# Two low-rank products of a recurrent layer's preparation parted, z tiles evacuated at an earlier due time, and one set of small transfers moved to another queue

## The chip, the cores and the metric

One core of a Trainium2 chip. The metric is the device time of one execution in microseconds (us), as the median of several runs. Engines are named as the profile names them: PE (TensorE: matmuls and transposes), PEld (its weight loads), DVE (VectorE), ACT (ScalarE), POOL (GpSimd) and SP (SyncE, which here only issues transfers). Each engine works through its own list of instructions in order; transfers can be issued from SP, ACT or POOL.

## The reference

A decoder layer for 1024 tokens of width 2048, in float32. One RMS norm feeds one input projection of 6528 columns. Its columns go to two groups of heads:

```python
h = rms_norm(x, norm_w[l], NORM_EPS)
z = h @ w_in[l]
y_rwkv = rwkv7_mixer(z[..., :RWKV_COLS], ...)   # 16 heads x 64
y_att = swa_sink_mixer(z[..., RWKV_COLS:], ...)  # 16 query heads, 2 key heads, window 128
x = x + concat([y_rwkv, y_att]) @ w_out[l]
```

The first group mixes each column with the token before it and then runs a recurrence per head, of which the parts that matter here are

```python
w = -softplus(-(w0 + tanh(wl) @ w2)) - 0.5
decay = exp(-exp(w))
a = sigmoid(a0 + al @ a2)
kk = k * k_k / norm(k * k_k)          # per head
k = k * (1 + (a - 1) * k_a)
# per token t: sa = state @ (-kk)
# state = state * decay + outer(sa, kk * a) + outer(v, k);  o = state @ r
```

`wl` and `al` have 64 columns each: `tanh(wl) @ w2` and `al @ a2` are the two low-rank products of the change.

## The kernel before

The tokens are worked through in two halves of 512 (`hf`). In each half a stream of z tiles is projected: a z tile is 128 output columns by 512 tokens, made in one of two PSUM banks (tag "z") by 48 matmuls of 128x128 by 512, as three products of high and low parts over 16 pieces of the contraction (L346, L347, L351). Weights come in four pieces per tile on SP (L335), are rounded by ACT to the high part `wh` (L321) and subtracted by POOL to the low part `wl` (L322).

A finished z tile is multiplied in its bank by the row norms (L353, DVE). `shifted` then blends it with the token before: ACT L359, DVE L360, ACT L361 and L362 (`zlast`, the last reader of the bank). Only then is the bank free for the tile after the next.

A unit (`unit`, 8 per half, so 16 in all) has six z tiles, in this order: k, r, v and the gate of two recurrent heads (`zk`, `zr`, `zv`, `zg`), then the queries of two attention heads, then the attention's gate. Beside the stream run generators for each unit:

- `rwkv_prep`: the two low-rank products (L390, L391, two matmuls each; the second operand of each is a low part), their tanh on ACT (L393, L394), the decay's cumulated sum `sig` (POOL L395, DVE scan L399) and its exponentials `Pc` and `Pi` (ACT L401, L405), `kmul` (ACT L397), the norm of kk through `headsum` (ACT L552, POOL L553, two matmuls L555 and L556; DVE L409 and the reciprocal L410), then the scaled operands `Gt` (L421, L422) and `F` (L426, L427). Per set of four chunks of 64 tokens 16 small matmuls follow (L436) into two banks; DVE masks them out of the banks into `Eab`, `BE` and `F` (L439, L440, L442). There are two sets, and both use the tag "m".
- `solve`, inside it: the inverse of each 16x16 triangle on DVE (L463, L464), copied out by ACT (L465), put into DRAM in two transfers (L467) and read back in four as larger blocks `dg` (L469), transposed by DVE (L473), and used in small matmuls from L477 to L512. Both sets of transfers are issued on SP.
- `rwkv_chain` (the recurrence over eight chunks, L578 to L589), `rwkv_post` (norm over each head, transposes L616), and `att` (attention of the unit; its last products are L724 and L726 with DVE L731, its output's transposes L735 with DVE L737). These of one unit run beside the next unit's `rwkv_prep`.

PSUM tag "m" has three banks for all of this. In `rwkv_prep` `pw` and `pa`, the banks of the two low-rank products, are taken together and then `pn` for the norm; `pa` is used on until L422.

What sets the order: `yield t` gives the due time of what follows, in planned us, and `at(t)` sets the same as a priority directly. A planner orders each engine's list at build time by due time among what its own cost model holds to be ready; on the chip the lists are fixed. A z tile is planned at 15.36 us (`TILE`), so a unit at 92.16; counted from its start `t0`, the low-rank products are due at 18.5, the norm sum at 23.2, `Gt` and `F` at 32, the L436 and masks at 57.2 (the second set's L436 and masks at 62.4), and a tile's evacuation at the planned end of the tile: 46.08 for `zv` and 61.44 for `zg`.

At the turn from the first half to the second, `hprep` loads, transposes (L287) and splits the second half of x (L262, L263), and the last unit's `solve` stands there without z tiles of the same half beside it. The x loads (L254) and weight loads (L335) are on SP, as L467 and L469.

Of the kernel before, what the change touches and what calls it, by code (L numbers as in the profile page):

```python
# [13 lines left out]
AF = mybir.ActivationFunctionType  # L14
ALU = mybir.AluOpType
# [49 lines left out]
def layer(tc, x, norm_w, w_in, w_out, mu_rwkv, w0, w2, a0, a2, k_k, k_a, r_k, lnx_w, lnx_b,  # L65
          q_norm_w, k_norm_w, sinks, rel_bias, cst, out, groups=range(NP), do_out=True, dbg=None):
    nc = tc.nc
# [5 lines left out]
    V, A, G, PE = nc.vector, nc.scalar, nc.gpsimd, nc.tensor  # L73

    def sb(shape, tag, bufs=1, dt=F32):
        return pool.tile(list(shape), dt, name=tag, tag=tag, bufs=bufs)

    HR = (slice(0, 64), slice(64, 128))
    NT = dict(t=4, ta=5, zt=5, wr=4, wh=3, wl=3)

    def tmp(tag="t"):
        return sb([P, T], tag, NT.get(tag, 1))

    def ps(tag, shape=(P, 512)):
        return psum.tile(list(shape), F32, name=tag, tag=tag, bufs={"z": 2, "m": 3, "o": 1, "ch": 1}[tag])
# [6 lines left out]
    def at(t):  # L92
        tc.cur_priority = 100000 + int(t * 1000)
# [15 lines left out]
    order, now = itertools.count(), [0.0]  # L109
# [42 lines left out]
    def col(name, i=0):  # L152
        return cols(name, 1, i)
# [14 lines left out]
    dv = {}  # L168
# [51 lines left out]
    dg, mp = sb([P, NC, 32], "dg"), sb([P, NC, 32], "mp")  # L220
    V.memset(dg[:], 0.0)
    xd = dram.tile([2, 2, NC, 32, 32], F32, name="xd", tag="xd")
    x5 = xd[:]
# [101 lines left out]
    def ztile(h, c0, c1=None):  # L325

        hh, hl, R = h
        z = ps("z")

        def load(q):  # L330
            def f(raw):
                r3 = raw.rearrange("p (k c) -> p k c", k=4)
                for i, c in ((slice(0, P), c0),) if c1 is None else ((HR[0], c0), (HR[1], c1)):
                    w = w_in[0, q * 512:(q + 1) * 512, c:c + i.stop - i.start]
                    nc.sync.dma_start(r3[:, :, i], w.rearrange("(k p) c -> p k c", p=P))  # L335
            return f

        t0 = clk[0]
        clk[0] += TILE
        for q in range(4):  # L340
            hi, lo = wpiece(load(q), t0 + q * 12 * MM)
            for k in range(4):
                kk = q * 4 + k
                yield t0 + (q * 12 + 2 * k) * MM
                wh = hi[:, k * P:(k + 1) * P]
                PE.matmul(z[:], lhsT=wh, rhs=hh[kk][:], start=(kk == 0), stop=False)  # L346
                PE.matmul(z[:], lhsT=wh, rhs=hl[kk][:], start=False, stop=False)  # L347
            for k in range(4):
                kk = q * 4 + k
                yield t0 + (q * 12 + 8 + k) * MM  # L350
                PE.matmul(z[:], lhsT=lo[:, k * P:(k + 1) * P], rhs=hh[kk][:], start=False, stop=(kk == KT - 1))  # L351
        yield clk[0]
        V.tensor_tensor(z[:], z[:], R[:], ALU.mult)  # L353
        return z

# [10 lines left out]
    def v3(t, n=T):  # L366
        return t.rearrange("p (c t) -> p c t", c=NC)

    def rwkv_prep(t0, hf, p, S, lor, zk, zr, zv):
# [10 lines left out]
        for i in range(2):  # L380
            hr = HR[1 - i]
# [2 lines left out]

        sq = tmp()
        A.activation(sq[:], zk[:, 0:T], AF.Square, scale=col("kk", p))
        pw, pa = ps("m"), ps("m")
        yield t0 + 18.5
        for i, (b, hr) in enumerate(zip((pw, pa), HR)):
            PE.matmul(b[:], lhsT=wla[:, i, :], rhs=lor[i][:], start=True, stop=False)  # L390
            PE.matmul(b[:], lhsT=whz[:, i, :], rhs=lor[2][:], start=False, stop=True)  # L391
        th = tmp()
        A.activation(th[:], pw[:], AF.Tanh, bias=dv["hw0"][:, p:p + 1], scale=0.5)  # L393
        A.activation(pa[:], pa[:], AF.Tanh, bias=dv["ha0"][:, p:p + 1], scale=0.5)  # L394
        G.tensor_scalar(sig[:, :, 1:65], v3(th[:]), 0.5, 0.5, ALU.mult, ALU.add)  # L395
        kmul = tmp()
        A.activation(kmul[:], pa[:], AF.Identity, bias=dv["cka"][:, p:p + 1], scale=dv["hka"][:, p:p + 1])  # L397
        fl = lambda t: t[:].rearrange("p a b -> p (a b)")
        V.tensor_tensor_scan(fl(sig), fl(rmask), fl(sig), 0.0, ALU.mult, ALU.add)  # L399
        Pc = sb([P, NC, 65], "Pc", 1)  # L400
# [2 lines left out]
        A.copy(pe[:], Pc[:, :, 64])  # L403
        Pi = tmp()
        A.activation(v3(Pi[:]), sig[:, :, 1:65], AF.Exp, scale=C0)  # L405
        pn = ps("m")
        yield from headsum(pn, sq, t0 + 23.2)
        n2 = tmp()
        V.tensor_scalar(n2[:], pn[:], 1e-24, None, ALU.max)  # L409
        V.reciprocal(n2[:], n2[:])  # L410
        V.scalar_tensor_tensor(pa[:], pa[:], 1.0, n2[:], ALU.add, ALU.mult)
        k3, r3 = v3(zk[:, 0:T]), v3(zr[:, 0:T])
        kP = Pi
# [37 lines left out]
        Xs = sb([64, 16, 16], "X")  # L451
# [3 lines left out]
        def solve():  # L455
            G.memset(Xs[:].rearrange("p s t -> p (s t)")[:, 0:256:17], 1.0)
            X = chx[0:64, 256:512].rearrange("p (s t) -> p s t", s=16)
            A.copy(X, Xs[:])  # L458
            for j in range(14, 0, -1):
                n = 15 - j  # L460
                yield t0 + 65 + n * 0.35
                q = sb([64, 64], "pr", 2)[:, 0:j * n].rearrange("p (s t) -> p s t", s=j)
                V.tensor_tensor(q, Xs[:, 0:j, j:j + 1].to_broadcast([64, j, n]), X[:, j:j + 1, j + 1:16].to_broadcast([64, j, n]), ALU.mult)  # L463
                V.tensor_tensor(X[:, 0:j, j + 1:16], X[:, 0:j, j + 1:16], q, ALU.add)  # L464
            A.copy(Xs[:], X)  # L465
            for x, h in halves:
                nc.sync.dma_start(x5.rearrange("i b c s t -> (i b c) s t")[:, h, h], Xs[x])  # L467
            for i, b, r, cb in quads:
                nc.sync.dma_start(dg[r], x5[i, b].rearrange("c s t -> s c t"))  # L469

            yield t0 + 77.5
            dt = sb([P, NC, 32], "k1", 2)
            V.transpose(dt[:], dg[:])  # L473
            pm = ps("m", (P, NC, 64))
            for c in range(NC):
                for i, b, r, cb in quads:
                    PE.matmul(pm[r, c, 0:32], lhsT=Eab[r, c, cb], rhs=dt[r, c, :], start=True, stop=True)  # L477
            V.copy_predicated(mp[:], low_i[:, None, :].to_broadcast([P, NC, 32]), pm[:, :, 0:32])
            yield t0 + 80.5
            for c in range(NC):  # L480
                for i, b, r, cb in quads:
                    PE.matmul(pm[r, c, 32:64], lhsT=dg[r, c, :], rhs=mp[r, c, :], start=True, stop=True)
            for i, b, r, cb in quads:
                A.copy(yt[r, :, r], pm[r, :, 32:64])

            yield t0 + 83
            x22 = sb([P, NC, 32], "k1", 2)
            pz = ps("m", (P, NC, 64))
            for c in range(NC):
                for i in range(2):  # L490
                    r0 = i * 64
                    PE.matmul(pz[r0 + 32:r0 + 64, c, 0:32], lhsT=Eab[r0:r0 + 32, c, 32:64], rhs=yt[r0:r0 + 32, c, r0:r0 + 32], start=True, stop=True)
            z1 = sb([P, NC, 32], "k1", 2)
            for i in range(2):
                r = slice(i * 64 + 32, i * 64 + 64)
                V.transpose(x22[r], yt[r, :, r])
                A.copy(z1[r], pz[r, :, 0:32])
            yield t0 + 85.5
            for c in range(NC):
                for i in range(2):  # L500
                    r = slice(i * 64 + 32, i * 64 + 64)
                    PE.matmul(pz[r, c, 32:64], lhsT=x22[r, c, :], rhs=z1[r, c, :], start=True, stop=True)
            for i in range(2):
                r0 = i * 64
                A.copy(yt[r0 + 32:r0 + 64, :, r0:r0 + 32], pz[r0 + 32:r0 + 64, :, 32:64])

            yield t0 + 88.5
            for c0 in (0, 4):
                cc = slice(c0, c0 + 4)
                b = ps("m", (P, 4, P))  # L510
                for c in range(4):
                    PE.matmul(b[:, c, :], lhsT=yt[:, c0 + c, :], rhs=BE[:, c0 + c, :], start=True, stop=True)  # L512
                for i, hr in enumerate(HR):
                    A.copy(bk[hr, cc, hr], b[hr, :, hr])
                    V.tensor_copy(Erb[hr, cc, HR[1 - i]], b[hr, :, HR[1 - i]])
# [4 lines left out]
        for c0 in (0, 4):  # L520
            b = ps("m", (P, 4, P))
# [27 lines left out]
    def headsum(acc, v, t):  # L549

        hi, lo = sb([P, T], "vh", 1, F32R), sb([P, T], "vl", 1, F32R)
        A.copy(hi[:], v[:])  # L552
        G.tensor_tensor(lo[:], v[:], hi[:].bitcast(F32), ALU.subtract)  # L553
        yield t
        PE.matmul(acc[:], lhsT=bonr[:], rhs=hi[:], start=True, stop=False)  # L555
        PE.matmul(acc[:], lhsT=bonr[:], rhs=lo[:], start=False, stop=True)  # L556
# [66 lines left out]

    def att_kv(hf, h):
        z = yield from ztile(h, RWKV_COLS + 1024)
        kz = tmp("ta")
        A.copy(kz[:], z[:])
# [225 lines left out]
    if dbg is not None:  # L853
        for hf in range(NH):
            for k in list(groups) + [NP + g for g in groups]:
                t = tmp()
# [28 lines left out]
```

## Time and profile before

| | |
|---|---|
| Median of 3 runs | 2073.68 us (2072.9 to 2077.31) |
| The profiled execution | 2074.8 us; span of its instructions 2073.0 us |
| PE busy | 1990.7 us (96%) |
| DVE busy | 1138.2 us (55%) |
| ACT busy | 1042.0 us (50%) |
| POOL busy | 858.0 us (41%) |
| Mean granted clock of PE | 0.989 |

The span runs from the first to the last instruction of the profiled execution. Busy times are sums over the engine's instructions. Matmuls overlap in the array, so a busy PE is not PE at its peak; idle time of PE is real. "a <- b" in a wait means that a stood until b had ended.

### The profile page before, as it was taken

To read this page: it belongs to the slowest core of one execution; us is meant where nothing else is said; L and a number is where in the kernel's file an instruction comes from. 1 tells how busy PE (TensorE), PEld (TensorE's weight loads), DVE (VectorE), ACT (ScalarE), POOL (GpSimd) and SP (SyncE) were. 2 spreads that over 40 slices of the span, in tenths; PEclk is the share of its full clock that TensorE was granted. 3 is DMA by queue.
4 is the path that set the end of the run, shared out by engine and by line. 5 is a ranking of instruction groups with operands and counts; after the bars stand their busy time and mean duration, and the time that the engine had idled before them with its cause. 6 is when DMAs were issued, how large, how long until landed. Compare 5 with 4: busy or idle time off the path is not lost.

```text
span 2073.0 us, 36509 instructions
## 1 busy us (share of the span) xinstructions
PE 1990.7 (96%) x13216; PEld 1632.8 (79%) x13216; DVE 1138.2 (55%) x2680; ACT 1042.0 (50%) x2563; POOL 858.0 (41%) x740
## 2 busy tenths in 40 slices
PE   7999999999999998899999999999999988999999
PEld 5778777787778786777878787877887778988887
DVE  5647575757574756676565665757575772011001
ACT  5445555565555564655645464555556562223221
POOL 4543434434353534144443534344343423444443
PEclk9999999999999999899999999999999999999999
DMA  7332323233332325123232324232323353455443
GB/s 181 88 89 65 93 64 82 76 79 75 81 80 77 87 65 153 42 84 82 78 79 64 96 56 100 62 92 68 81 75 78 75 167 121 152 157 171 134 136 117
DMA packets 412293, 197.02 MB, mean 95 GB/s; under 512 B 216941, under 2 KB 381136, under 8 KB 412112
## 3 DMA queue, kind: packets, MB, share of 16 engines
q1 hardware_dynamic: 371360, 181.90, 32.0%
q10 hardware_dynamic: 40000, 11.67, 2.3%
q0 software_dynamic: 752, 1.11, 0.5%
q8 instruction: 104, 1.70, 0.3%
q14 instruction: 77, 0.63, 0.1%
HBM read 173.51 MB, written 21.10 MB: 94 GB/s over the span
## 4 chain that ended last, share of the span: by engine, by line
PE 38%; DVE 9%; issue 3%; POOL 1%; ACT 1%; DMA 1%; SPq 0%; POOLq 0%; ACTq 0%
PE z L346 6%; PE z L347 6%; PE z L351 6%; PE z L787 2%; PE z L789 2%; PE z L788 2%; PE m L789 2%; PE m L788 2%; PE m L787 2%; POOL wl L322 1%; DVE t L410 1%; PE o L789 1%; PE o L788 1%; PE o L787 1%; PE o L578 1%
## 5 line engine op out<-in xcount | busy, mean ns | idle before, releaser
L322 POOL TENSOR_TENSOR wl<-wr,wh 128x512 fp32r<-128x512 f32 x536 | 707.6, 1324 | 979.9 <-ACT wh L321 510.1
L346 PE MATMUL z<-hh,wh 128*128 128x512 f32 x1632 | 665.1, 408 | 9.7 <-ACT zlast L362 7.6
L347 PE MATMUL z<-hl,wh 128*128 128x512 f32 x1632 | 650.4, 398 | 0.0
L321 ACT CAST wh<-wr 128x512 fp32r<-128x512 f32 x536 | 331.2, 619 | 581.9 <-PE z L347 213.6
L351 PE MATMUL z<-hh,wl 128*128 128x512 f32 x1632 | 477.3, 405 | 0.0
L346 PEld LDWEIGHTS z<-hh,wh 128*128 128x128 f32 x1632 | 308.7, 189 | 81.6 <-ACT zlast L362 13.3
L347 PEld LDWEIGHTS z<-hl,wh 128*128 128x128 f32 x1632 | 308.9, 189 | 59.4 <-DVE hl L263 0.3
L351 PEld LDWEIGHTS z<-hh,wl 128*128 128x128 f32 x1632 | 297.4, 189 | 59.3 <-issue 0.2
L353 DVE TENSOR_TENSOR z<-z,R 128x512 f32<-128x512 f32 x102 | 70.9, 695 | 135.4 <-PE z L351 132.0
L787 PE MATMUL z<-wh,hh 128*128 128x256 f32 (+1 forms) x352 | 113.5, 323 | 11.5 <-ACT hh L259 5.8
L581 ACT ACTIVATE s<-svu,pe 64x64 f32<-64x64 f32 x256 | 88.3, 345 | 49.9 <-DVE svu L589 46.1
L788 PE MATMUL z<-wl,hh 128*128 128x256 f32 (+1 forms) x352 | 112.5, 320 | 0.0
L789 PE MATMUL z<-wh,hl 128*128 128x256 f32 (+1 forms) x352 | 112.5, 320 | 0.0
L578 PEld LDWEIGHTS o<-svu,F 128*128 128x128 f32 x512 | 79.7, 189 | 26.4 <-DVE svu L589 16.5
L589 DVE SCALAR_TENSOR_TENSOR svu<-ch,pe,s 64x64 f32<-64x64 f32 x224 | 63.2, 282 | 65.5 <-PE ch L585 61.7
L463 DVE TENSOR_TENSOR pr<-X,ch 64x14 f32<-64x14 f32 (+6 forms) x224 | 42.3, 189 | 99.8 <-ACT ch L458 92.8
L578 PE MATMUL o<-svu,F 128*128 128x64 f32 x512 | 82.7, 265 | 7.6 <-DVE svu L589 7.1
L787 PEld LDWEIGHTS z<-wh,hh 128*128 128x128 f32 x352 | 68.5, 195 | 16.7 <-ACT hh L259 6.2
L795 DVE TENSOR_TENSOR ta<-z,ta 128x256 f32<-128x256 f32 (+1 forms) x22 | 9.9, 493 | 127.6 <-PE z L789 127.6
L795 DVE TENSOR_TENSOR ta<-m,ta 128x512 f32<-128x512 f32 x9 | 6.1, 689 | 124.8 <-PE m L789 124.8
L788 PEld LDWEIGHTS z<-wl,hh 128*128 128x128 f32 x352 | 68.7, 195 | 4.3
L789 PEld LDWEIGHTS z<-wh,hl 128*128 128x128 f32 x352 | 68.6, 195 | 4.3
(278 smaller groups left out, 3351.6 us busy)
## 6 DMA issues: line engine op xcount, KB each, us to landing
wr<-in_w_in SPq DMA_DIRECT2D x280, 256.0 KB, 2.9
wr<-in_w_in SPq DMA_DIRECT2D x256, 128.0 KB, 2.6
wr<-in_w_out SPq DMA_DIRECT2D x64, 256.0 KB, 2.9
wr<-in_w_out SPq DMA_DIRECT2D x128, 128.0 KB, 2.9
ta<-in_x SPq DMA_DIRECT2D x37, 256.0 KB, 5.4
zt<-yd SPq DMA_DIRECT2D x32, 256.0 KB, 3.7
out<-ta SPq DMA_DIRECT2D x24, 256.0 KB, 4.0
yd<-ta ACTq DMA_DIRECT2D x16, 256.0 KB, 3.0
```

The source lines that it names most:

```text
L321: A.copy(hi[:], raw)
L322: G.tensor_tensor(lo[:], raw, hi[:].bitcast(F32), ALU.subtract)
L346: PE.matmul(z[:], lhsT=wh, rhs=hh[kk][:], start=(kk == 0), stop=False)
L347: PE.matmul(z[:], lhsT=wh, rhs=hl[kk][:], start=False, stop=False)
L351: PE.matmul(z[:], lhsT=lo[:, k * P:(k + 1) * P], rhs=hh[kk][:], start=False, stop=(kk == KT - 1))
L353: V.tensor_tensor(z[:], z[:], R[:], ALU.mult)
L578: PE.matmul(O[:, c, i, :], lhsT=F[c // 4][:, i, c % 4, :], rhs=svu[:, i, c, :], start=c % 4 == 0 and i == 0, stop=False, skip_group_check= ...
L581: A.activation(s0[hr], svu[hr, i, c, :], AF.Copy, scale=pe[hr, c:c + 1])
L589: V.scalar_tensor_tensor(dst, ch[hr, i, :], pe[hr, c:c + 1], s0[hr], ALU.mult, ALU.add)
L787: PE.matmul(o, lhsT=yh[k][:, ts], rhs=wh, start=k == 0 and tt % n == 0, stop=False, skip_group_check=True)
L788: PE.matmul(o, lhsT=yh[k][:, ts], rhs=wl, start=False, stop=False, skip_group_check=True)
L789: PE.matmul(o, lhsT=yl[k][:, ts], rhs=wh, start=False, stop=k == KT - 1 and tt % n == n - 1, skip_group_check=True)
```

## The change

The evacuation of every z tile, and what directly follows it, gets a due time 14 us earlier. In `rwkv_prep` the two low-rank products no longer stand together: the first is due at 17.5, then come the norm sum (due at 21.5) with its reciprocal, the scan and the exponentials, and the second product with its tanh and `kmul` is due at 27; each takes its bank at its own place. The transfers L467 and L469 of the last unit of the first half go through POOL's queue in place of SP's.

```diff
@@ ztile
         yield clk[0]
+        at(now[0] - 14)
         V.tensor_tensor(z[:], z[:], R[:], ALU.mult)
@@ rwkv_prep
-        pw, pa = ps("m"), ps("m")
-        yield t0 + 18.5
-        for i, (b, hr) in enumerate(zip((pw, pa), HR)):
+
+        def lora(i):
+            b = ps("m")
             PE.matmul(b[:], lhsT=wla[:, i, :], rhs=lor[i][:], start=True, stop=False)
             PE.matmul(b[:], lhsT=whz[:, i, :], rhs=lor[2][:], start=False, stop=True)
+            return b
+
+        yield t0 + 17.5
+        pw = lora(0)
         th = tmp()
         A.activation(th[:], pw[:], AF.Tanh, bias=dv["hw0"][:, p:p + 1], scale=0.5)
-        A.activation(pa[:], pa[:], AF.Tanh, bias=dv["ha0"][:, p:p + 1], scale=0.5)
         G.tensor_scalar(sig[:, :, 1:65], v3(th[:]), 0.5, 0.5, ALU.mult, ALU.add)
-        kmul = tmp()
-        A.activation(kmul[:], pa[:], AF.Identity, bias=dv["cka"][:, p:p + 1], scale=dv["hka"][:, p:p + 1])
+        pn = ps("m")
+        yield from headsum(pn, sq, t0 + 21.5)
+        n2 = tmp()
+        V.tensor_scalar(n2[:], pn[:], 1e-24, None, ALU.max)
+        V.reciprocal(n2[:], n2[:])
         fl = lambda t: t[:].rearrange("p a b -> p (a b)")
         V.tensor_tensor_scan(fl(sig), fl(rmask), fl(sig), 0.0, ALU.mult, ALU.add)
...
         A.activation(v3(Pi[:]), sig[:, :, 1:65], AF.Exp, scale=C0)
-        pn = ps("m")
-        yield from headsum(pn, sq, t0 + 23.2)
-        n2 = tmp()
-        V.tensor_scalar(n2[:], pn[:], 1e-24, None, ALU.max)
-        V.reciprocal(n2[:], n2[:])
+        yield t0 + 27
+        pa = lora(1)
+        A.activation(pa[:], pa[:], AF.Tanh, bias=dv["ha0"][:, p:p + 1], scale=0.5)
+        kmul = tmp()
+        A.activation(kmul[:], pa[:], AF.Identity, bias=dv["cka"][:, p:p + 1], scale=dv["hka"][:, p:p + 1])
         V.scalar_tensor_tensor(pa[:], pa[:], 1.0, n2[:], ALU.add, ALU.mult)
@@ solve
+            q = nc.gpsimd if hf == 0 and p == groups[-1] else nc.sync
             for x, h in halves:
-                nc.sync.dma_start(x5.rearrange("i b c s t -> (i b c) s t")[:, h, h], Xs[x])
+                q.dma_start(x5.rearrange("i b c s t -> (i b c) s t")[:, h, h], Xs[x])
             for i, b, r, cb in quads:
-                nc.sync.dma_start(dg[r], x5[i, b].rearrange("c s t -> s c t"))
+                q.dma_start(dg[r], x5[i, b].rearrange("c s t -> s c t"))
```

## Rows read from the trace of the kernel before

**Rows 1.** The page's busy us, share of the span, instructions, by engine

```profile
PE 1990.7 (96%) x13216; PEld 1632.8 (79%) x13216; DVE 1138.2 (55%) x2680; ACT 1042.0 (50%) x2563; POOL 858.0 (41%) x740
```

**Rows 2.** Windows of 20 us: length, busy us (instructions), granted clock, DMA share, GB/s

```profile
820.00:840.00 20.00, 7.26 (x203) 5.48 (x203) 3.16 (x6) 5.32 (x14) 2.49 (x2) 0.64 0.43 109
...
1340.00:1360.00 20.00, 18.61 (x107) 14.58 (x106) 18.91 (x37) 7.50 (x16) 7.49 (x7) 1.00 0.40 99
```

**Rows 3.** Waits of PE, whole span: us in total, times, longest us

```profile
PE m L436 <- DVE F L442: 12.4, 20, 1.9
PE m L477 <- DVE k L473: 10.1, 1, 10.1
...
PE z L346 <- ACT zlast L362: 7.6, 13, 0.8
```

**Rows 4.** Timeline of PE, a unit of the second half: start, us, instruction [idle before]

```profile
1328.20 0.48 PE L390 MATMUL m<-lr,wla 128*128 128x512 f32 x1
...
1329.21 0.33 PE L726 MATMUL m<-vt,ta 128*128 128x64 f32 x2
...
1348.80 1.10 PE L351 MATMUL z<-hh,wl 128*128 128x512 f32 x4
1350.19 0.50 PE L346 MATMUL z<-hh,wh 128*128 128x512 f32 x1 [0.29 <-ACT zlast L362]
...
1353.38 1.13 PE L436 MATMUL m<-F,Gt 64*128 64x128 f32 x14 [0.92 <-DVE F L442]
```

**Rows 5.** Timeline of DVE in the same unit

```profile
1332.71 0.42 DVE L731 TENSOR_TENSOR ta<-m,sm 128x256 f32<-128x256 f32 x1 [0.92 <-PE m L726]
...
1336.72 3.35 DVE L410 RECIPROCAL t<-t 128x512 f32<-128x512 f32 x1
...
1347.36 0.70 DVE L353 TENSOR_TENSOR z<-z,R 128x512 f32<-128x512 f32 x1
...
1350.41 0.41 DVE L439 TENSOR_TENSOR Eab<-m,tri 64x256 f32<-64x256 f32 x1
...
1352.55 0.68 DVE L442 TENSOR_TENSOR F<-m,tri 64x512 f32<-64x512 f32 x1
1353.16 0.68 DVE L353 TENSOR_TENSOR z<-z,R 128x512 f32<-128x512 f32 x1
```

**Rows 6.** Timeline of all engines, the last unit of the first half

```profile
791.05 0.70 DVE L353 TENSOR_TENSOR z<-z,R 128x512 f32<-128x512 f32 x1
...
792.51 0.39 ACT L361 ACTIVATE zv<-zlast,zv,par 128x1 f32<-128x1 f32 x1
...
793.37 0.74 DVE L360 SCALAR_TENSOR_TENSOR zv<-z,par,zv 128x511 f32<-128x511 f32 x1
...
794.41 0.50 PE L346 MATMUL z<-hh,wh 128*128 128x512 f32 x1 [0.82 <-ACT zlast L362]
```

**Rows 7.** Timeline of all engines at the turn

```profile
821.61 0.36 ACT L465 COPY X<-ch 64x256 f32<-64x256 f32 x1
...
821.78 2.49 POOL L322 TENSOR_TENSOR wl<-wr,wh 128x512 fp32r<-128x512 f32 x2 [4.02 <-ACT wh L321]
...
823.53 0.99 SPq L467 DMA_DIRECT2D xd<-X  x2
...
826.85 1.81 SPq L469 DMA_DIRECT2D dg<-xd  x4
831.12 0.45 DVE L473 STREAM_TRANSPOSE k<-dg 128x256 f32<-128x256 f32 x1 [8.80 <-DMA dg<-xd]
```

**Rows 8.** Transfers by issuing queue: count, KB each, median us from issue to landing

```profile
dg<-xd SPq DMA_DIRECT2D x64, 32.0 KB, 2.3
...
bias_d<-Eab POOLq DMA_DIRECT2D x1, 1024.0 KB, 12.6
...
xd<-X SPq DMA_DIRECT2D x32, 32.0 KB, 2.8
...
bia<-in_q_norm_w POOLq DMA_DIRECT2D x2, 0.2 KB, 3.4
```

## The prediction

> **What bounds the kernel now.** I read the page's busy times first, then the windows, then TensorE's waits, and last the instructions of one unit and of the turn between the two token halves. TensorE (PE) is busy 1990.7 of 2073.0 us [rows 1], so only its 82 idle us can be won; the change removes no matmul. In a steady 20 us window inside a unit PE lacks 1.4 us, and DVE is at 18.91 of 20 there; in the window of the turn PE is busy 7.26 us and its granted clock is 0.64 on average, so much of it at the lower of the two levels (1.2 instead of 2.4 GHz) while PE stands idle [rows 2]. The waits say where the rest lies: 12.4 us in 20 waits of the second set of chunk products (L436) for a mask on DVE (L442), 10.1 us in one wait of L477 for a transpose on DVE (L473), and 7.6 us in 13 waits of a new z tile for the evacuation of an old one (L362) [rows 3].
>
> In one unit it looks so. PE ends the gate's z tile (zg) at 1349.90, is held 0.29 us before the next tile because the bank of zv is not empty, goes on, and is held again 0.92 us before the L436 that starts at 1353.38 [rows 4]. The other side is DVE: it stood 0.92 us until 1332.71 for PE (L731), then worked without a gap through the reciprocal (3.35 us), evacuated zv only at 1347.36, though PE had long left that tile, reached the masks at 1350.41 and ended them at 1352.55 + 0.68 = 1353.23 [rows 5]. So the end of the second L442 on DVE sets when PE goes on. A unit of the first half has the same shape with a longer z wait, 0.82 us [rows 6].
>
> **The two low-rank products parted.** Before, four matmuls stand together from 1328.20 to 1329.21, 1.01 us, ahead of the rest of the attention product that DVE's L731 waits for [rows 4, 5]. The second pair leaves that place, so L731 and all DVE work chained behind it can start about 0.5 us earlier. The pair itself costs the same 0.5 us of PE wherever it stands: no gain, no loss in PE work. Its tanh and kmul on ACT come later; they are needed by L411 and L421, which stand behind the reciprocal, and its 3.35 us hide them (the tanh and the affine step are under 1 us each). If that cover were gone, L421 would be about 1 us late and the masks with it. The norm sum and its reciprocal move ahead of the scan in the text; DVE has no gap between them before, so this is an exchange within one full engine and I cost it at nothing; it could give up to the 0.92 us that DVE stood idle, if the scan no longer has to stand behind L731, or take as much if the scan then waits behind the reciprocal. The third gain that one could claim, a PSUM bank held some us shorter, frees nothing that a wait of PE names, so nothing.
>
> Sum of this part: the masks end 0.5 us earlier in each of 15 units, -7.5 us; bounds 0 and 15 x 0.92 = -13.8, the whole idle time of DVE.
>
> **z tiles evacuated first.** All evacuations now carry a due time 14 us earlier; on DVE and ACT that puts them ahead of what is due up to 14 us before. For zv: in the early unit its last input on ACT is ready at 792.51 + 0.39 = 792.90, but DVE takes L360 only at 793.37, 0.47 us later, behind other work [rows 6]; going first returns these 0.47, and the 0.5 us of lead from the parted products covers the rest of the 0.82, as it covers the 0.29 of the later half. 7 waits of 0.82 and 6 of 0.29 make 7.5, the 7.6 of the row [rows 3, 4, 6]. But each stands a few us ahead of a mask wait, and a PE that comes earlier waits longer there. I take three quarters, -5.7 us; bounds 0 and -7.6.
>
> The same rule works against the masks. The tile zg, due 61.44 us after the unit's start, is now due at 47.44, and the masks at 57.2: its multiplication (L353, 0.68 us), which before ran at 1353.16 behind the masks [rows 5], can now stand ahead of or between them. PE ends zg at 1349.90 and DVE, with its lead, would reach the masks at 1349.91: the two meet, so I count it in half of the units, 15 x 0.34 = +5.1 us. Bounds: 0, and 15 x (0.68 + 0.74) = +21.3 if the L360 of zg (its price by the early unit's row) passes them too.
>
> **Inverses through POOL's queue at the turn.** One unit of 16 is touched, with six transfers. Before, the inverse is copied out at 821.61 + 0.36 = 821.97 and SP issues the first transfer only at 823.53, 1.56 us late, as it stands behind a weight load; the second set goes out at 826.85, DVE's transpose follows at 831.12, and PE has nothing else in its list for 10.1 us [rows 3, 7]. POOL is in two weight subtractions from 821.78 to 824.27 [rows 7]. Behind the first of them (at 823.0) the transfers would start 0.5 us earlier than on SP; behind both, 0.74 later; at once, 1.56 earlier. What a POOL issue of 32 KB takes to land no row shows. The small ones took 3.4 us, against medians of 2.8 and 2.3 on SP; the large one, 1 MB, 12.6 [rows 8]. The size is nearest to the small ones: 0.6 + 1.1 = 1.7 us slower in two hops, less the 0.5: +1.2 us. Bounds: -1.6 (landing as on SP, issued at once) and, by the 12.6 for both hops, about +20. What is queued behind: POOL's weight subtractions wait while a second hop waits for the first, and SP's next weight loads wait for them; PE stands idle there, so this stays hidden unless the wait outlasts the stretch up to the next half's first z products. SP's own queue is freed of six issues; nothing that PE waits for stands behind them.
>
> The rows have POOL's small transfers slower by 0.6 to 1.1 us a hop [rows 8]. The Trainium skill (DMA: Bandwidth & Descriptors, sections "Issuing engine by pattern" and "Latency and other measured facts") says the same for another reason: a plain load or store belongs on the Sync queue, whose descriptors hardware makes, with a first byte at about 0.6 us, against about 1 us where GpSimd writes them. By that page the two hops would cost 0.8 us more, an estimate, and the turn +0.3 instead of +1.2.
>
> **The sum.** -7.5 - 5.7 + 5.1 + 1.2 = -6.9 us against the profiled execution's 2074.8 us (span 2073.0 and 1.8 around it): 2067.9. That execution lies 1.1 us above the median of 2073.68, so the median forecast is 2066.8 us.
>
> **Rivals.**
> *The waits are only handed on (no change).* DVE's amount of work before the second L442 is the same, and the zv wait is followed by the mask wait. If zg's L353 passes the masks in every unit (+10.2) and the z waits give nothing by themselves, -7.5 + 10.2 + 1.2 = +3.9, and if it passes in a third, -7.5 + 3.4 + 1.2 = -2.9: 2070.8 to 2077.6, about 2073 to 2074. For it: DVE is the full engine there. Against: PE's list is laid out anew, and a free z bank lets z products stand ahead of L436.
>
> *z first passes the masks altogether (slower).* L353 and L360 of zg ahead of the second L442: 1.42 - 0.5 = 0.92 us more per unit, 13.8; less 5.7, plus 1.2: +9.3, 2083.0 us. It decides from 1.07 us of evacuation per unit ahead of the masks (15 x 1.07 = 16.1, less 7.5 and 5.7, plus 1.2, is the 4.1 us that a measurement can tell). For it: the order of due times, 47.44 before 57.2. Against: L360 needs ACT's two steps behind L353, some 2 us, by which time the second masks have begun.
>
> *All waits of the units go (much faster).* 12.4 + 7.6 = 20 us off, less the turn's +1.2: 2054.9. It needs DVE some 1.4 us earlier at the masks, more than the 0.92 us that it stood idle; only a better place of L436 in PE's list gives it.
>
> *The new queue does not do what it should.* It is in the sum with its loss; only with the far bound (+20) would it decide by itself, 2085; little speaks for that, as 32 KB is no megabyte.
>
> **How the numbers follow.** Small gain as summed 0.45 (2058 to 2069.5), all waits gone 0.08 (2050 to 2058), handed on 0.25, masks passed 0.22. A measurement of this kernel can tell about 0.2% from no change. So faster 0.53, same 0.25, slower 0.22. The range, 2051 to 2083, reaches from the all-gone case to the passed masks.
>
> **What would show it.** Right: the zlast wait is gone from PE's waits, DVE's idle before L731 is about 0.4 us, the mask wait per unit is at or under 1 us, L473 at the turn comes within 2 us of its distance from the inverse's copy (9.2 us). Wrong: a mask wait of 1.5 us or more with L353 of zg ahead of L442; a new wait of L351 for POOL's subtraction; L421 waiting for kmul; or a gap at the turn that shrinks or grows by several us, which would mean that a queue or PE's list there is other than I read it.

## The result, and the profile after

The changed kernel takes 2093.39 us (median of 4 runs, 2088.33 to 2094.09) where the kernel before took 2073.29 beside it: a ratio of 1.0090, 95% interval 1.0067 to 1.0113. It is slower by 0.9%, 18.6 us by the ratio. The forecast was 2066.8.

The page's line of busy times, after (beside [rows 1]):

```profile
PE 2003.0 (96%) x13216; PEld 1635.5 (78%) x13216; DVE 1141.7 (55%) x2680; ACT 1039.3 (50%) x2563; POOL 863.3 (41%) x746
```

PE runs the same 13216 matmuls and is busy 12.3 us longer; the other 6.3 us of the longer span (2091.6 against 2073.0) are idle time. Where does the loss fall? Every unit has one scan on DVE (sums along the tokens, here of the decay), so the way from scan to scan is a unit's length. Two stretches are plain, without the turn in them: six units of the first half ("early") and five of the second ("late"). These are the scans (L406) at the start and the end of either, after:

```profile
195.64 1.24 DVE L406 TENSOR_TENSOR_SCAN sig<-rmask,sig 128x520 f32<-128x520 bf16 x1
...
783.64 1.24 DVE L406 TENSOR_TENSOR_SCAN sig<-rmask,sig 128x520 f32<-128x520 bf16 x1
...
1146.67 1.23 DVE L406 TENSOR_TENSOR_SCAN sig<-rmask,sig 128x520 f32<-128x520 bf16 x1
...
1642.42 1.23 DVE L406 TENSOR_TENSOR_SCAN sig<-rmask,sig 128x520 f32<-128x520 bf16 x1
```

and the same four of the kernel before (its L399):

```profile
193.65 1.61 DVE L399 TENSOR_TENSOR_SCAN sig<-rmask,sig 128x520 f32<-128x520 bf16 x1
...
776.29 1.62 DVE L399 TENSOR_TENSOR_SCAN sig<-rmask,sig 128x520 f32<-128x520 bf16 x1
...
1138.99 1.23 DVE L399 TENSOR_TENSOR_SCAN sig<-rmask,sig 128x520 f32<-128x520 bf16 x1
...
1623.94 1.23 DVE L399 TENSOR_TENSOR_SCAN sig<-rmask,sig 128x520 f32<-128x520 bf16 x1
```

The six early units together take 588.0 us after and 582.6 before: +5.4. The late ones take 495.75 and 484.95: +10.8, or 99.2 us a unit instead of 97.0. Up to the first scan +2.0; from 783.64 to 1146.67, the turn and the units around it, 363.0 against 362.7; behind the last scan +0.1. So the loss lies in the plain units, and more than half of it in the five late ones.

PE's waits after, over the whole span (us in total, times, longest us; beside [rows 3]):

```profile
PE m L443 <- DVE F L449: 11.7, 20, 0.9
PE m L486 <- DVE k L482: 8.7, 1, 8.7
...
PE m L625 <- DVE t L621: 7.2, 7, 1.8
PE z L346 <- ACT zlast L363: 6.4, 13, 0.7
...
PE m L443 <- DVE F L434: 1.7, 7, 0.3
```

The z wait (L346) is not gone. The mask wait is as it was, and two waits are new: the output's transposes (L625) for the head norm's last product on DVE, and the first chunk products for a factor F (L434). One late unit on DVE, after (timeline; beside [rows 5]):

```profile
1542.99 0.76 DVE L740 TENSOR_TENSOR ta<-m,sm 128x256 f32<-128x256 f32 x2 [0.87 <-PE m L735]
...
1546.59 3.33 DVE L404 RECIPROCAL t<-t 128x512 f32<-128x512 f32 x1
1549.85 0.62 DVE L421 TENSOR_TENSOR t<-zt,t 128x512 f32<-128x512 f32 x1
...
1553.88 1.51 DVE L434 TENSOR_TENSOR F<-zt,Pc 64x256 f32<-64x256 f32 x1
...
1555.82 0.42 DVE L434 TENSOR_TENSOR F<-zt,Pc 64x256 f32<-64x256 f32 x1
...
1564.18 0.68 DVE L449 TENSOR_TENSOR F<-m,tri 64x512 f32<-64x512 f32 x1
```

and on POOL in the same stretch:

```profile
1550.61 1.28 POOL L428 TENSOR_TENSOR Gt<-t 64x512 f32<-64x512 f32 x1 [1.05 <-DVE t L421]
1551.97 1.63 POOL L322 TENSOR_TENSOR wl<-wr,wh 128x512 fp32r<-128x512 f32 x1
1553.81 1.29 POOL L322 TENSOR_TENSOR wl<-wr,wh 128x512 fp32r<-128x512 f32 x1 [0.22 <-PE z L351]
```

DVE now takes the reciprocal ahead of the key's multiplication (L421), which stood first before (L414). So POOL's half of Gt, which needs that multiplication, starts 6.9 us behind the scan (1543.67) instead of 3.9. The second of POOL's weight subtractions behind it starts at 1553.81, 0.07 us ahead of DVE's F (L434). That F takes 1.51 us; its twin at 1555.82, with POOL idle, takes 0.42. The first F ends 0.29 us behind the end of POOL's subtraction (1555.10). The Trainium skill (SBUF — State Buffer, section "SBUF: two separate sides") has a rule for it: a DVE instruction with two SBUF inputs and a GpSimd instruction that reads SBUF take the same pair of ports, and whichever starts second stands until the first is done. The trace agrees roughly: 1.22 us of POOL's instruction were left when F began, which with F's own 0.42 makes 1.64, and it took 1.51.

Which of the two moved? In a late unit it is F. This is the late unit of [rows 5] before, DVE and POOL:

```profile
1342.56 1.50 DVE L422 SCALAR_TENSOR_TENSOR Gt<-t,hkk,m 64x512 f32<-64x512 f32 x2
1344.08 0.53 DVE L427 TENSOR_TENSOR F<-zt,Pc 64x256 f32<-64x256 f32 x1
...
1343.04 1.29 POOL L322 TENSOR_TENSOR wl<-wr,wh 128x512 fp32r<-128x512 f32 x1 [1.94 <-PE z L351]
```

POOL's subtraction waited for PE in both kernels and stands 10.0 us behind the scan before, 10.1 after. F started 11.0 us behind the scan before and 10.2 after, so POOL now meets F where it met L422, which reads one operand (`m`) from PSUM and took the same 1.50 us in both. In one of the five late units (scan at 1246.96) POOL comes 0.3 us later still and meets the next product of F, which then takes 1.41 us instead of 0.48. In an early unit it is POOL that moved (after, POOL and DVE):

```profile
597.56 2.87 POOL L322 TENSOR_TENSOR wl<-wr,wh 128x512 fp32r<-128x512 f32 x2
...
599.47 1.24 DVE L434 TENSOR_TENSOR F<-zt,Pc 64x256 f32<-64x256 f32 x1
```

Here the subtractions follow POOL's half of Gt without a gap and start 9.1 us behind the scan instead of 6.1.

The end of the second mask comes 25.91 us behind the first low-rank product (1538.95 to 1564.18 + 0.68), against 25.03 before (1328.20 to 1353.23, [rows 4, 5]): 0.9 us later, not 0.5 earlier. From L740 (L731 before) to that end is 21.87 us instead of 20.52, 1.35 more: 0.98 are in the four products of F, 0.42 in the small steps of the head norm (L241 to L243), of which seven stand there instead of five. The lead of L740 behind the first product, 0.47, takes part of it back. What comes 44 us later in the same unit is the other half of the loss (all engines, timeline):

```profile
1606.93 0.38 PE L594 MATMUL ch<-svu,k 128*128 128x128 f32 x2
...
1607.77 0.68 DVE L354 TENSOR_TENSOR z<-z,R 128x512 f32<-128x512 f32 x1
...
1608.94 0.60 DVE L598 SCALAR_TENSOR_TENSOR svu<-ch,pe,s 64x64 f32<-64x64 f32 x2
...
1609.30 0.40 PE L587 MATMUL o<-svu,F 128*128 128x64 f32 x2
```

The same place of a late unit before:

```profile
1392.85 0.70 DVE L353 TENSOR_TENSOR z<-z,R 128x512 f32<-128x512 f32 x1 [3.21 <-PE z L351]
...
1396.71 0.38 PE L585 MATMUL ch<-svu,k 128*128 128x128 f32 x2
...
1397.13 0.28 DVE L589 SCALAR_TENSOR_TENSOR svu<-ch,pe,s 64x64 f32<-64x64 f32 x1 [0.85 <-PE ch L585]
```

This is the recurrence's first state update. Before, zk of the next unit was evacuated 4.3 us ahead of it, and the update began 0.42 us behind its matmul. After, PE ends the zk tile just ahead of that matmul, the evacuation (L354) goes first on DVE, and the update begins 2.01 us behind its matmul. So it is in all five late units (2.00 to 2.01), and 0.42 in all five before.

At the turn (ACT, POOL and DVE, after; beside [rows 7]):

```profile
829.45 0.36 ACT L472 COPY X<-ch 64x256 f32<-64x256 f32 x1
...
830.86 1.38 POOL L476 DMA_DIRECT2D xd<-X  x2
...
835.84 2.30 POOL L478 DMA_DIRECT2D dg<-xd  x4 [2.32 <-issue]
839.79 0.45 DVE L482 STREAM_TRANSPOSE k<-dg 128x256 f32<-128x256 f32 x1 [7.34 <-DMA dg<-xd]
```

From the copy's end (829.81) to the transpose 9.98 us, against 9.15 before (821.97 to 831.12).

Last, the granted clock, the share of its full speed that TensorE was given. Its mean over the span is 0.985 after and 0.989 before. Times the spans, 31.4 and 22.8 us of full clock were not granted: up to 8.6 of the 18.6 us. Two of the eleven plain units hold a stretch at the lower level (1.2 GHz), one of them here (windows: length, busy us of PE, PEld, DVE, ACT, POOL, then granted clock, DMA share, GB/s):

```profile
1160.00:1168.30 8.30, 6.29 (x36) 4.28 (x34) 8.06 (x20) 2.63 (x5) 4.52 (x4) 1.00 0.37 97
1168.35:1171.75 3.40, 3.40 (x19) 2.79 (x16) 3.39 (x8) 2.44 (x6) 0.46 (x1) 0.50 0.31 95
```

PE had stood idle 2.0 of 8.3 us, for the z tile and the masks, before the clock fell. That unit took 100.3 us, the other late ones 98.5 to 99.4; the other such unit, an early one, 99.1, its neighbours 97.7 and 97.8. PE idles 2.0 us at that place in the other four late units too and 1.8 us in all six early ones; but for the two, all keep the full clock there. Before it idles 1.4 to 1.5 us there, and no plain unit holds such a stretch. The two stretches make 3.4 of the 8.6 us; the rest lies at the start and about the turn.

### The profile page after: what moved, and what is told of

Same layout as the page of the kernel before. It is cut to its first block, busy times and chain, and to the rows that moved or that the text cites. A ratio compares the mean times of both kernels' runs of the same rounds, so it can differ in the third digit from the quotient of the medians.

```text
span 2091.6 us, 36555 instructions
## 1 busy us (share of the span) xinstructions
PE 2003.0 (96%) x13216; PEld 1635.5 (78%) x13216; DVE 1141.7 (55%) x2680; ACT 1039.3 (50%) x2563; POOL 863.3 (41%) x746
## 4 chain that ended last, share of the span: by engine, by line
PE 42%; DVE 5%; issue 3%; ACT 2%; POOL 1%; DMA 1%; ACTq 0%; SPq 0%; POOLq 0%
PE z L346 7%; PE z L351 7%; PE z L347 6%; PE z L798 2%; PE z L796 2%; PE z L797 2%; PE m L798 2%; PE m L796 2%; PE m L797 2%; PE o L796 1%; PE o L798 1%; PE o L797 1%; POOL wl L322 1%; PE ch L594 1%; PE o L587 1%
## 5 line engine op out<-in xcount | busy, mean ns | idle before, releaser
L346 PE MATMUL z<-hh,wh 128*128 128x512 f32 x1632 | 669.2, 410 | 9.1 <-ACT zlast L363 6.4
L346 PEld LDWEIGHTS z<-hh,wh 128*128 128x128 f32 x1632 | 309.4, 190 | 80.5 <-ACT zlast L363 12.1
L354 DVE TENSOR_TENSOR z<-z,R 128x512 f32<-128x512 f32 x102 | 70.9, 695 | 127.6 <-PE z L351 125.1
```

## The experiments

Times are medians; each ratio is to the kernel before, run on the same chip (2072.97 us for the first four kernels, 2073.75 for the next four, 2074.0 for the last four). The first four take the change apart; theory A was that the parting does the harm, B that z first does, C that the queue does.

**z first alone**, on the kernel before:

```diff
         yield clk[0]
+        at(now[0] - 14)
         V.tensor_tensor(z[:], z[:], R[:], ALU.mult)
```

> The kernel before with the earlier due time of the z evacuations alone. Theory A (the parted preparation does the harm: kP comes behind the reciprocal on DVE and kmul comes late, so POOL makes its half of Gt later and its weight subtractions run beside DVE's operations with two SBUF inputs, which are stretched): this one lies within 4 us of before. Theory B (the evacuations, going first on DVE and ACT, push the head norm of rwkv_post and the chain's steps back): 8 to 15 us slower, with a wait of the output transposes for the head norm.

2073.81 us, 0.9997 (0.9988 to 1.0006): no change. The z wait fell from 7.6 to 4.0 us, and the mask wait grew from 12.4 to 15.1. What the one gives, the other takes.

**The parting alone**, the prep's lines of the change on the kernel before, without z first and with SyncE's queue:

```diff
-        pw, pa = ps("m"), ps("m")
-        yield t0 + 18.5
...
+        yield t0 + 17.5
+        pw = lora(0)
...
+        yield from headsum(pn, sq, t0 + 21.5)
...
+        V.reciprocal(n2[:], n2[:])
...
         V.tensor_tensor_scan(fl(sig), fl(rmask), fl(sig), 0.0, ALU.mult, ALU.add)
...
+        yield t0 + 27
+        pa = lora(1)
```

> The kernel before with the parted low-rank products and the earlier norm sum alone. Theory A: 14 to 19 us slower, nearly all of the whole change, and the second L442 ends some 1.3 us later after DVE's attention step than in before, with an F operation stretched from 0.4 to over 1 us. Theory B: within 5 us of before.

2081.88 us, 1.0037 (1.0024 to 1.0050): +7.7 us, half of what theory A wrote and more than theory B did. The stretched F is there in both halves, and the second mask ends 0.6 (early) to 0.7 us (late) later behind the first product. The early units take 97.4 to 97.8 us, the late ones 97.1 to 98.0.

**POOL's queue alone**, on the kernel before:

```diff
+            q = nc.gpsimd if hf == 0 and p == groups[-1] else nc.sync
             for x, h in halves:
-                nc.sync.dma_start(x5.rearrange("i b c s t -> (i b c) s t")[:, h, h], Xs[x])
+                q.dma_start(x5.rearrange("i b c s t -> (i b c) s t")[:, h, h], Xs[x])
             for i, b, r, cb in quads:
-                nc.sync.dma_start(dg[r], x5[i, b].rearrange("c s t -> s c t"))
+                q.dma_start(dg[r], x5[i, b].rearrange("c s t -> s c t"))
```

> The kernel before with the six transfers of the turn on POOL's queue alone. Theories A and B: within 3 us of before, as the stretch from the last unit of the first half to the second of the second half is 260.6 us in before and 260.9 with the whole change. Rival C (the queue at the turn does a good part of the harm): 5 us slower or more, with a longer wait of PE for the transposed blocks.

2070.78 us, 0.9982 (0.9973 to 0.9991): 3.7 us faster, a version better than both kernels. Its wait of L478 at the turn is 10.4 us, no shorter; the gain is not there. In the unit behind the turn (from 911.6 to 1034.2 us, 122.6 instead of 123.9 long) PE's mask wait, before

```profile
PE m L436 <- DVE F L442: 1.9, 1, 1.9
```

and with POOL's queue

```profile
PE m L436 <- DVE F L442: 0.7, 1, 0.7
```

is 1.2 us shorter. From the last scan of the first half to 1034.2 the two profiled executions differ by 1.9 us (258.8 and 260.6); the rest of the 3.7 was not located.

**The whole change with the reciprocal behind the key's multiplication** in the text:

```diff
         V.tensor_scalar(n2[:], pn[:], 1e-24, None, ALU.max)
-        V.reciprocal(n2[:], n2[:])
...
-        V.scalar_tensor_tensor(pa[:], pa[:], 1.0, n2[:], ALU.add, ALU.mult)
...
         V.tensor_tensor(kP[:], zk[:, 0:T], Pi[:], ALU.mult)
+        V.reciprocal(n2[:], n2[:])
+        V.scalar_tensor_tensor(pa[:], pa[:], 1.0, n2[:], ALU.add, ALU.mult)
```

> The whole change, but the reciprocal stands behind kP on DVE again. Theory A: POOL's half of Gt starts about 1 us earlier and 3 to 15 us of the loss come back. Theory B: no change against the whole change, about 20 us slower than before.

2089.11 us, 1.0077 (1.0063 to 1.0091): 2.7 us of the loss are back by the ratios, just short of theory A's 3 to 15, and the intervals of the two overlap. The trace says more. In the early half the order turned, F's four products take 1.7 us again instead of 2.5, and five of six units are back at 96.9 to 97.2 us. In the late half the planner still put the reciprocal ahead, and the units stayed at 98.8 to 100.2.

The three parts make 0 + 7.7 - 3.7 = +4, not +18.6. So they meet. The next four tell which, with the theory of the zk tile (D) against a part of the queue in it (E).

**Parting and z first, SyncE's queue**:

```diff
-            q = nc.gpsimd if hf == 0 and p == groups[-1] else nc.sync
+            q = nc.sync
```

> The changed kernel with the inverse's transfers back on SyncE's queue: parting and z first together, the two parts that alone gave +8 and 0. Theory D (the two parts meet: parting moves the end of the zk tile, the first of the next unit, in TensorE's stream in the late half, from 5 us before the recurrence's first state update to beside it, and z first then lets its evacuation of 0.68 us and its mixing of 0.75 us go ahead of that update; about +1.6 us in each of five units of the late half, and some short stretches of the lower clock besides): 2091 to 2097, late units 98.5 to 99.5. Rival E (the POOL queue is the partner, it costs only beside the parted products): about 2082, late units 97.2.

2090.96 us, 1.0081 (1.0068 to 1.0094); late units 98.6 to 99.9. That is what theory D wrote, a little low in the total and high in the units.

**Parting and POOL's queue**, the changed kernel without z first:

```diff
-        at(now[0] - 14)
```

> The changed kernel without z first: parting and POOL's queue. Theory D: the zk evacuation stays behind the first state update, so the time is that of parting alone less what the queue gave alone, 2076 to 2080; late units 97.2 to 97.9. Rival E: the harm of the whole is here, 2088 to 2093, late units 98.5.

2080.97 us, 1.0035 (1.0023 to 1.0047). This is theory D's number within 1 us, and far from rival E's; the queue gives nothing beside the parting. Late units 97.2 to 97.7, but one of 99.4 that holds a stretch of 3.4 us at the lower clock.

**z first and POOL's queue**, products not parted (the two edits above on the kernel before):

> The kernel before with z first and POOL's queue, products not parted. Both theories: no interaction, 2069 to 2072, as with the queue alone; if z first harms in any company, 2075 or more.

2070.22 us, 0.9988 (0.9979 to 0.9996). So parting and z first meet: on the unparted kernel z first costs 0, on the parted one 1.0081 - 1.0037 = 0.44%, 9 us. Rival E falls, as the queue costs nothing beside the parting. But its gain of 3.7 us is not there beside the parting either (1.0035 against 1.0037), a difference at the edge of what the intervals can tell.

**The whole change, zk alone evacuated in its turn**:

```diff
-    def ztile(h, c0, c1=None):
+    def ztile(h, c0, c1=None, ahead=14):
...
-        at(now[0] - 14)
+        at(now[0] - ahead)
...
-        zk = yield from shifted(h, 8 + p)
+        zk = yield from shifted(h, 8 + p, ahead=0)
```

> The whole change, but the zk tile alone evacuated in its turn (no advance of 14 us); all other z tiles first. Theory D: the first state update is issued ahead of zk's evacuation again, late units back at 97.2 to 97.9, the time 2080 to 2086. Rival E: unchanged, 2091 to 2095. A third theory, that the stretched subtraction of F beside POOL is what costs in the late half, also leaves it unchanged, since the subtraction stays where it is.

2088.4 us, 1.0063 (1.0051 to 1.0076): 5.6 us of the loss are back, less than theory D wrote. The order is the expected one: the state update begins 0.83 us behind its matmul in every late unit. So it does in the two parted kernels without z first; wherever the parting and z first stand together, zk going first, it is 2.0 us or more, and on the unparted kernel with z first 0.42. The late units without a clock stretch take 97.7 and 98.2 us, down from 98.5 to 99.4. But the other three hold a stretch at the lower clock and take 98.7 to 99.3. The delay of the masks is still in this kernel, and with it the clock's part.

The last four go at what delays the masks (F: the early norm; G: the late second product), and at what a delay costs (K).

**The second product right behind the first**, norm early as in the change:

```diff
         G.tensor_scalar(sig[:, :, 1:65], v3(th[:]), 0.5, 0.5, ALU.mult, ALU.add)
+        pa = lora(1)
+        A.activation(pa[:], pa[:], AF.Tanh, bias=dv["ha0"][:, p:p + 1], scale=0.5)
...
-        yield t0 + 27
-        pa = lora(1)
```

> The whole change with the second low-rank product and its multiplier issued right behind the first one instead of 9.5 us of planned time later; the norm stays early. Theory F (the early norm does the harm in the early half: its 3.35 us reciprocal goes ahead of the key's multiplication, so POOL's half of Gt and POOL's next subtraction come late and stretch F's product): no help, early units stay at 97.5 to 97.8, F's four products at 2.5 us, 2089 to 2095. Rival G (the late second product holds Gt up): early units back at 97.0, 2084 to 2089. Late units stay near 98.7 by both.

2087.93 us, 1.0058 (1.0046 to 1.0070). Theory F was wrong in its detail. F's early products are not stretched (1.7 us in five of six units), and still the early units take 97.6 to 98.3. Another instruction with two SBUF inputs now meets POOL, the key's multiplication (one early unit, DVE's timeline):

```profile
591.99 3.34 DVE L408 RECIPROCAL t<-t 128x512 f32<-128x512 f32 x1
595.25 1.41 DVE L420 TENSOR_TENSOR t<-zt,t 128x512 f32<-128x512 f32 x1
```

POOL is in a weight subtraction from 594.83 to 596.12. The gain of 6.6 us by the ratios goes in part with the clock (0.990 on average, no stretch in a plain unit); it was not traced further.

**The norm back behind the exponentials**, all else as changed:

```diff
-        pn = ps("m")
-        yield from headsum(pn, sq, t0 + 21.5)
-        n2 = tmp()
-        V.tensor_scalar(n2[:], pn[:], 1e-24, None, ALU.max)
-        V.reciprocal(n2[:], n2[:])
...
         A.activation(v3(Pi[:]), sig[:, :, 1:65], AF.Exp, scale=C0)
+        pn = ps("m")
+        yield from headsum(pn, sq, t0 + 23.2)
+        n2 = tmp()
+        V.tensor_scalar(n2[:], pn[:], 1e-24, None, ALU.max)
+        V.reciprocal(n2[:], n2[:])
```

> The whole change with the norm's sum and reciprocal back behind the exponentials, at the planned time of the kernel before; the products stay parted, z first and POOL's queue stay. Theory F with D: F's products back at 1.7 us in both halves, TensorE's idle time ahead of the second mask back at 1.3 to 1.6 us from 2.0, no stretch of the lower clock inside a unit; early units 97.0; but late units still 98 or more, since zk's evacuation is still ahead of the first state update; 2080 to 2085. Rival G (the late second product): early units stay at 97.6, 2089 or more.

2078.38 us, 1.0016 (1.0007 to 1.0026): 15 us back by moving the reciprocal with its norm sum. Rival G falls: the second product is as late here as in the change, and the early units are back. One late unit on DVE:

```profile
1529.81 0.68 DVE L421 TENSOR_TENSOR t<-zt,t 128x512 f32<-128x512 f32 x1
1530.40 3.35 DVE L412 RECIPROCAL t<-t 128x512 f32<-128x512 f32 x1
...
1537.54 0.46 DVE L434 TENSOR_TENSOR F<-zt,Pc 64x256 f32<-64x256 f32 x1
```

and POOL beside it:

```profile
1530.66 1.29 POOL L428 TENSOR_TENSOR Gt<-t 64x512 f32<-64x512 f32 x1 [1.80 <-DVE t L421]
1532.03 2.54 POOL L322 TENSOR_TENSOR wl<-wr,wh 128x512 fp32r<-128x512 f32 x2
```

POOL's half of Gt and most of two subtractions run while DVE is in the reciprocal, which has one input and is not stretched: 3.35 us here, 3.33 and 3.34 above, whatever POOL does. PE idles 1.3 to 1.6 us ahead of the masks' end instead of 1.8 to 2.0, and no plain unit holds a stretch of the lower clock (mean 0.990). The early units are back at 96.8 to 97.3, the late ones at 97.8 to 98.6.

**The same, with zk in its turn** (both edits):

> The run before this with zk's tile alone evacuated in its turn as well: both harms undone. Theory F with D: early units 97.0, late units 97.0 to 97.4, the kernel level with z first and POOL's queue on the kernel before, 2070 to 2076. If parting harms in a third way, 2080 or more.

2073.42 us, 0.9994 (0.9983 to 1.0005). The late units are at 96.9 to 97.4. The recurrence's start in one of them, PE and DVE:

```profile
1586.89 0.38 PE L594 MATMUL ch<-svu,k 128*128 128x128 f32 x2
...
1587.72 0.59 DVE L598 SCALAR_TENSOR_TENSOR svu<-ch,pe,s 64x64 f32<-64x64 f32 x2
...
1589.58 0.70 DVE L354 TENSOR_TENSOR z<-z,R 128x512 f32<-128x512 f32 x1
```

The update begins 0.83 us behind its matmul instead of 2.01, and zk follows. With these two undone nothing is left of the loss that can be measured, and nothing of a gain either.

**The kernel before with its masks made late** by one multiplication by 1.0:

```diff
+            if c0 == 0:
+                V.tensor_scalar(bs[0][:], bs[0][:], 1.0, None, ALU.mult)
             for (i, hr), b in zip(enumerate(HR), bs):
```

> The kernel before with one multiplication by 1.0 more on VectorE, in place on the first PSUM bank of each unit's first products, ahead of the masks: about 0.65 us more on the way to the masks and nothing else. Theory K (a later mask leaves TensorE idle 0.6 us longer there, about 2.0 us instead of 1.4, and in some units the granted clock then falls to half for 3.4 us, at 1.5 us each): units 97.5 to 97.7 without and 99 with such a stretch, in total plus 8 to plus 16 us. Rival L (slack behind the masks takes it up, the clock stays): 2073 to 2076.

2099.5 us, 1.0120 (1.0104 to 1.0136): +25 us for 16 instructions of 0.68 us, 11 us in all. PE's mask wait:

```profile
PE m L436 <- DVE F L444: 22.7, 27, 1.9
```

It grew by 10.3 us over the 12.4 of [rows 3]. Four of eleven plain units hold a stretch at the lower clock, as this one of the late half; the next late unit, with nearly the same idle time, holds none (windows, columns as above):

```profile
1360.70:1368.90 8.20, 5.97 (x35) 4.23 (x33) 8.07 (x18) 2.63 (x5) 4.66 (x4) 1.00 0.42 107
1368.95:1372.30 3.35, 3.35 (x17) 2.84 (x18) 3.35 (x7) 2.79 (x7) 0.31 (x1) 0.50 0.09 19
1459.90:1468.10 8.20, 6.17 (x38) 4.39 (x34) 8.07 (x19) 2.63 (x5) 4.49 (x4) 1.00 0.42 108
1468.20:1471.60 3.40, 3.32 (x24) 2.83 (x25) 3.40 (x7) 2.71 (x7) 0.44 (x1) 1.00 0.15 33
```

The first takes 99.4 us, the second 98.0: a stretch costs 1.4 us. The mean clock is 0.986, so 6.5 us more than before were not granted (2094.6 x 0.014 - 22.8). Theory K holds in kind, with a higher price than it wrote. The early units without a stretch take 98.6 to 99.4 us instead of 97.1; why they lose more than the late ones was not traced.

## Why the prediction was wrong

**The products parted (-7.5 forecast, +7.7 measured alone).** The lead is there: L740 starts 4.04 us behind the first product (1542.99 - 1538.95), L731 before started 4.51 behind it [rows 4, 5], though the scan, which now stands behind both L740, gains only 0.13 (4.72 against 4.85). What failed is the sentence that the norm's sum and reciprocal ahead of the scan are "an exchange within one full engine" at no cost. It is an exchange of order, and the reciprocal was the cover in which POOL did its two-input work. Put ahead of the key's multiplication, it covers less; POOL's half of Gt comes 3 us later, and POOL's subtractions fall beside F or the key's multiplication, in the early units because POOL is later, in the late ones because F is earlier; those stretch by 0.8 to 1.1 us. The bounds, 0 and -13.8, excluded any loss, although the text named a loss of up to 0.92 us a unit. The late tanh and kmul did no harm of their own, as forecast: DVE has no idle time from the scan to its half of Gt, and issuing them early did not bring the early units back.

**z tiles first (-5.7 and +5.1 forecast; 0 alone, +9 on the parted products).** The z wait fell only by half alone, and in the changed kernel from 7.6 to 6.4. zg did not pass the masks: L354 of zg ran at 1564.79, behind the second mask at 1564.18. That rival ("z first passes the masks altogether") ended on the right side for a wrong reason. The step looked at zv and zg alone. The tile that mattered is zk of the next unit, and it is the parting that made it matter: in the late half it moved the recurrence's first matmul from 6 z matmuls behind zk's end to right at it, so that an evacuation with an earlier due time went ahead of the state update. In five units an update 2.0 instead of 0.83 us behind its matmul makes 6 of the 9 us, an estimate from these rows; the rest is not located. The rival "handed on" is what z first does by itself.

**POOL's queue (+1.2 forecast).** The path from copy to transpose grew by 0.83 us, inside the bounds of -1.6 and +20 and within the 2 us named. The first issue came 0.51 us sooner behind the copy (1.05 instead of 1.56), as reckoned; but the first hop, from issue to issue, took 1.66 us more (4.98 against 3.32) and the second 0.32 less (3.95 against 4.27), where the sum had 0.6 and 1.1 more. The estimate by the Trainium skill (DMA: Bandwidth & Descriptors, section "Latency and other measured facts") was +0.3; the 0.83 lies between that and the 1.2. But alone the queue gained 3.7 us, of which 1.2 are a shorter mask wait behind the turn, a place that the step did not cost.

**The clock, which the sum did not hold.** PE's waits were priced at their own length. Their price is higher: a delay of 0.68 us at the masks cost 1.0 us in a late unit without a clock stretch (97.0 to 98.0), and 2.4 with one. It is not one price: with the parting alone the masks end 0.7 us later in the late units, and these took 0.1 to 1.0 us more. In the changed kernel up to 8.6 of the 18.6 us are granted clock, 3.4 of them in the plain units.

**What the runs settle.** Moving the norm back returns 0.74% (1.0090 to 1.0016), putting zk in its turn as well 0.22% more, to 0.9994. That the parting delays the masks through POOL and DVE side by side is read from timelines, not tried by itself: no kernel ran without POOL's subtractions. How much each mask delay costs in a unit is not settled either. Why the clock falls in one unit and not in its neighbour with nearly the same idle time stays open, and so does where 2.5 of the queue's 3.7 us come from.

## What to carry to other kernels

Before you move a long instruction within a full engine, ask what another engine does under its cover: two engines that slow each other make the order a cost of its own. An earlier due time for all evacuations moves each ahead of whatever is ready at the same moment, so look at every tile that it touches, above all beside a serial recurrence. Parts that cost 0 and 8 us alone cost 17 together here; try pairs, not only parts.

## What the runs showed of the hardware that was not expected

A DVE product with two SBUF inputs took 1.51 us instead of 0.42 beside a POOL subtraction of 128x512, and a reciprocal 3.33 to 3.35 us with POOL beside it or not. TensorE's granted clock fell to 0.50 for 3.4 us in one of five late units of the changed kernel, each with 2.0 us of idle time in 8.3 us ahead of it, and in one of six early ones with 1.8; in the kernel before, with 1.4 to 1.5 us there, in none. On the unparted kernel, POOL's queue carried the turn's six transfers of 32 KB in a path only about 0.6 us longer than SyncE's (9.77 us against 9.15), and the kernel was 3.7 us faster.
